# Low parts of the second feed-forward matrix: by an adding DMA in place of a subtraction on DVE

## The chip, the cores and the metric

The kernel runs on one core of one Trainium2 chip. The metric is the device time of one execution in microseconds (us). The core has a matrix engine (TensorE, PE, with its weight loads shown as PEld), a vector engine (VectorE, DVE), an activation engine (ScalarE, ACT), a general engine (GpSimd, POOL) and a synchronising engine (SyncE, SP) that issues most DMAs. Each engine works through its own list of instructions in order and waits for others by semaphores. Data lie in SBUF (128 partitions), matmul results in PSUM, weights in DRAM.

## The reference, cut to what matters

A trunk of two layers over 512 tokens with 1024 channels, all in float32. Each layer has four token mixers and then a feed-forward block, and the change is in the latter:

```
x = x + mixed @ w_out
h2 = rms_norm(x, norm_ff)
return x + jnp.square(jax.nn.relu(h2 @ w_ff1)) @ w_ff2      # w_ff1 [1024, 4096], w_ff2 [4096, 1024]
```

## The kernel before

**Three products for one.** PE multiplies in float32r, a shortened float32. To keep accuracy each operand is split in a high part (its float32r rounding) and a low part (what is left), and a product is the sum of high x high, low x high and high x low, added up in PSUM. So each block of weights is needed as `wh` (high) and `wl` (low).

**Weight chunks.** All weights are laid out in DRAM as one stream `w` of chunks [128, 1024] (512 KB), in the order of use. `chunk()` takes the next one. SP loads it into a raw buffer `wr` (three of them, `wr0` to `wr2`, in turn; seen as float32 they are called `wr0f`, as float32r `wr0r`). ACT copies it to `wh` (two buffers), which rounds it (line 275). DVE then writes raw - wh over the raw buffer (line 276): this is the low part.

**Use.** `mtile()` takes one chunk and makes 128 output channels for all 512 tokens: for k = 0 to 7 a matmul of `wh` with the high part of the activations, one of `wl` with the high part, and one of `wh` with the low part, 24 matmuls of 128x512. PE's order keeps these threes, so that the second matmul of a chunk is the first to need `wl`. In the trace both read as names of tiles: `ps<-yh,wh` or `ps<-yh,wr1r`.

**Feed-forward.** Four groups g in each layer. A group is 8 chunks of `w_ff1` (m = 0 to 7; relu and scale on DVE, line 475, square and high part on ACT, lines 476 and 478, low part on DVE, line 479) and then 8 chunks of `w_ff2`, whose results are added to x by DVE (line 485). That is 64 chunks of `w_ff2` in the program.

**What sets the order.** A scheduler writes each engine's list from the program's priorities and its own estimates of time; loads and splits of chunks have a raised priority. A load into a `wr` buffer waits until the chunk three before is done with on PE, a copy into a `wh` buffer until the one two before is. Beside the last group of `w_ff2` in layer 0 stand the first steps of layer 1's norm: ACT makes `hh` (line 370) and squares (line 338), POOL adds the squares (line 339). Beside that of layer 1 stand the squares of the last norm (line 388).

Of the kernel before, what the change touches and what calls it, by code (L numbers as in the profile page):

```python
# [32 lines left out]
# columns of the per-layer small pack  # L33
# [3 lines left out]
# columns of the constant pack  # L37
# [6 lines left out]
def fb(ap):  # L44
    return ap.bitcast(F32)


class Dual:
    """a buffer seen as float32 and as float32r"""
# [14 lines left out]
class Kern:  # L64
    def __init__(self, tc, A, out, depth, dbg=None):
        self.tc, self.nc, self.A, self.out, self.depth = tc, tc.nc, A, out, depth
        self.dbg = dbg or {}
        self.pools = []
        self.trace = None
        self.cidx = 0  # L70

# [110 lines left out]
    def setup_more(self):  # L182
# [24 lines left out]
        # second-pass key operands: rows 0-63 keys, then rows of -1 (64-95 or 96-127), zeros elsewhere  # L207
# [17 lines left out]
        # rope tables, rows as channels of two heads  # L225
# [29 lines left out]
    def order(self, a, b):  # L255
        """b after a on their engine"""
        self.tc.add_manual_dep(b.ins, a.ins.name,
                               mybir.DependencyInfo(mybir.DependencyClass.NoSync, mybir.DependencyReason.DATA),
                               reason="table order")
# [5 lines left out]
    def chunk(self, split=True):  # L265
        nc = self.nc
        i = self.cidx
        self.cidx += 1
        with self.tc.high_priority(4000 if i == 0 else 2000):
            raw = self.dual("wr")  # L270
            nc.sync.dma_start(raw.f[:], self.A["w"][i])
            if not split:
                return raw.f[:]
            wh = self.t("wh", 1024, F32R)
            nc.scalar.activation(wh[:], raw.f[:], AF.Copy)  # L275
            nc.vector.tensor_sub(raw[:], raw.f[:], fb(wh[:]))  # L276
        return wh, raw

    def mtile(self, xh, xl):
        """one tile of 128 output channels, transposed: [128 ch, 512 tok] in PSUM"""  # L280
        wh, wl = self.chunk()
        o = self.ps(self.dtag)
        n = len(xh)
        for k in range(n):
            s = slice(k * P, (k + 1) * P)
            self.mm(o[:], wh[:, s], xh[k][:], k == 0, False)
            self.mm(o[:], wl[:, s], xh[k][:], False, False)
            self.mm(o[:], wh[:, s], xl[k][:], False, k == n - 1)
        return o

    def mhalves(self, xh, xl):
        """mtile by halves of the tokens: (PSUM, tokens)"""
        wh, wl = self.chunk()
        for h in range(2):
            t = slice(h * 256, h * 256 + 256)
            o = self.ps(self.dtag, 256)
            for k in range(KT):
                s = slice(k * P, (k + 1) * P)
                self.mm(o[:], wh[:, s], xh[k][:, t], k == 0, False)
                self.mm(o[:], wl[:, s], xh[k][:, t], False, False)  # L300
                self.mm(o[:], wh[:, s], xl[k][:, t], False, k == KT - 1)
            yield o, t

    def vproducts(self, bank):
        """256 channels, token-major: two banks of two token tiles"""
        acc = [self.ps(bank) for _ in range(2)]
        for half in range(2):
            wh, wl = self.chunk()
            for k in range(4):
                for t in range(4):  # L310
                    o = acc[t // 2][:, (t % 2) * 256:(t % 2) * 256 + 256]
                    kk = half * 4 + k
                    s = slice(k * 256, (k + 1) * 256)
                    ts = slice(t * P, (t + 1) * P)
                    self.mm(o, self.hh[kk][:, ts], wh[:, s], kk == 0 and t % 2 == 0, False)
                    self.mm(o, self.hl[kk][:, ts], wh[:, s], False, False)
                    self.mm(o, self.hh[kk][:, ts], wl[:, s], False, kk == 7)
        return acc

    def vtiles(self, evac, acc=None):  # L320
        """evac(tok tile, psum [128 tok, 256 ch]) of the next 256 channels"""
        acc = acc or self.vproducts("d")
        with self.hi():
            for t in range(4):
                evac(t, acc[t // 2][:, (t % 2) * 256:(t % 2) * 256 + 256])

# [1 line left out]
    def rms(self, x, bank, early, in_psum=False):  # L328
        """x tiles -> 1/rms per token: [128, 512] (rows alike) and token-major [128, 4]"""
# [33 lines left out]
    def norm_split(self, x, gcol):  # L363
        """x * g as two parts; the tokens' 1/rms goes onto what is made of them"""
# [11 lines left out]
    def scaled(self, dst, o, scale=1.0):  # L376
        """dst = o * scale / rms"""
# [3 lines left out]
    def final(self, x):  # L381
        """the last norm; the last tile of channels comes in two halves of the tokens"""
# [36 lines left out]
    def layer(self, l, x):  # L419
# [5 lines left out]
        # the first products need no norm before they are written out  # L425
# [25 lines left out]
        # output projection  # L451
# [16 lines left out]
        for g in range(4):  # L468
            tags = rtags if g % 2 == 0 else rtags2
            RH, RL = [], []  # L470
            for m in range(8):
# [9 lines left out]
                RL.append(rl)  # L481
            for m in range(KT):
                last = l == self.depth - 1 and g == 3 and m == KT - 1
                for o, h in self.mhalves(RH, RL) if last else ((self.mtile(RH, RL), slice(0, S)),):
                    nc.vector.tensor_add(x[m][:, h], x[m][:, h], o[:])  # L485
        return x

    def ysplit(self, y):
        """y [128, 512] -> (high, low) tiles; the low part takes y's place"""
# [6 lines left out]
    def sigmoid(self, z):  # L496
        """in place, z at least -44"""
# [5 lines left out]
    def branch(self, n, qt):  # L503
        """mixed += sigmoid(gate_n + b) * (y_n @ W_branch_n), two tiles of channels"""
# [34 lines left out]
    def qk_pair(self, b_tiles=None):  # L539
        """project a pair of heads; per head (A, Q1, Q2) with  # L540
        head 0: A=[kh;kl], Q1=[qh;qh], Q2[0:64]=ql; head 1: A=[kl;kh], Q1=[qh;qh]; with b_tiles
        (rows 0-63 = kh) ql in Q2[0:64], else in the rows of kh"""
# [4 lines left out]
        out = []  # L547
# [11 lines left out]
    def kstack(self, k, A, B, b):  # L559
        """k on rows b*64..: its high part there in A, the low part in A's other half"""  # L560
# [7 lines left out]
    def regions(self, S3, win):  # L568
        """per key block: (psum AP, first query)"""
# [13 lines left out]
    def rowmax(self, S3, dst, win, negc=None):  # L583
        """column maxima of the masked scores; dst [32 rows, 512] gets diag(m)"""
# [35 lines left out]
    def probs(self, S3, win=False, bias=None, strict=False):  # L620
        """exp of the scores, masked; list of (AP, first query) per key block"""
# [19 lines left out]
    def pv(self, o, V, pr, start=True):  # L641
        """o [M, 512] += V_j^T P_j"""
# [3 lines left out]
    def recip(self, s, rows):  # L646
        """1/s for s [64 rows of PSUM], written at `rows`"""
# [7 lines left out]
    def v_plain(self, tag, c):  # L655
        """256 channels of values, token-major"""
# [6 lines left out]
    def sb_v(self, c, acc):  # L663
        """values of four heads, each as its high and low parts beside each other"""
# [17 lines left out]
    def sb_att(self, i):  # L682
        """scores with the queries on partitions, so that the sums over later keys are scans"""
# [3 lines left out]
        for b in range(2):  # L687
# [5 lines left out]
            # rows of 128 queries against all keys up to them: (bank, first column)  # L693
# [30 lines left out]
            # keys on partitions: (bank, first column) of a block of keys, queries from the same block on  # L724
# [27 lines left out]
    def vpair_evac(self, V, pair0):  # L752
        """token tile of 256 channels (4 heads) into [V0 | 1 | V1] groups of 192"""
# [15 lines left out]
    def small_proj(self):  # L769
        """nsa gates rows 0-23, gla decay rank rows 32-47, forget gate rows 64-71"""  # L770
# [16 lines left out]
        # gates of the three parts of the sparse attention, through DRAM to be read as rows alike  # L787
# [31 lines left out]
    def rope(self, o, scale, r=None):  # L819
        """rotated o * scale / rms, in r or in a tile of its own"""  # L820
# [11 lines left out]
    def compress_in(self, pecol):  # L832
        """two tiles [128 = (two positions, channel), 8 position pairs, 64 = (group, 31 blocks + pe)]"""
# [22 lines left out]
    def cmp_step(self, i, c):  # L856
        """a quarter of the first compression product"""
# [14 lines left out]
        if c == 3:  # L872
            # the position part
# [74 lines left out]
    def nsa(self, pi):  # L948
        """selected (here: all causal) and window attention of two heads"""
        nc = self.nc  # L950
        g, q, Ab, V = pi // 2, self.q, self.Ab, self.vnsa
        if True:
# [3 lines left out]
            for b in range(2):  # L956
# [7 lines left out]
                for br in range(2):  # L964
# [7 lines left out]
                    # [V|1] or [1|V] by the half the group's values sit in  # L972
# [17 lines left out]
    def nsa_cmp(self, g):  # L990
        """compressed attention of group g's four heads"""
# [40 lines left out]
    def gla_x(self, n, i):  # L1032
        """q (scaled) or k of two heads"""
# [7 lines left out]
    def gla_b(self, i):  # L1041
        """decays of two heads, summed within 64 tokens"""
# [25 lines left out]
    def gla(self, i):  # L1068
# [4 lines left out]
        if True:  # L1073
# [3 lines left out]
            # far pairs: products of decays from the middle of 512, 256 and 128 tokens  # L1077
# [47 lines left out]
            # pairs of one block of two tokens, the diagonal with them  # L1125
# [17 lines left out]
            # the other levels inside a block of 128 tokens; the two heads' queries beside each other,  # L1143
            # each with zeros at the other's channels
# [61 lines left out]
    def logsig(self, z, out):  # L1206
        """out = min(z, 0) - ln(1 + exp(-|z|))"""
# [10 lines left out]
def _kxm(w, c0):  # L1218
    """[K, 128 columns] -> [128, K/128 * 128]"""
# [11 lines left out]
# the token mixers' pieces in the order they are emitted: projections (with weights) and, in steps, attention  # L1231
# [142 lines left out]
```

## Time and profile before

| | |
|---|---|
| median of 3 runs | 2278.51 us (2278.09 to 2279.06) |
| profiled execution, span from first to last instruction | 2273.7 us |
| PE busy | 2230.2 us, 98% |
| DVE, ACT, POOL busy | 1488.2, 1035.6, 428.5 us |
| mean granted PE clock | 0.991 |
| DMA, mean | 90 GB/s |

The profile is one execution of the program. Its span leaves out what lies before the first and behind the last instruction, so it is 4.8 us below the median. Busy times of different engines overlap. A line of a group names the source line and engine, the tile written and the tiles read; behind "idle before" stands how long the engine stood still ahead of it, and which instruction ended that. Matmuls are pipelined, so that the time from one start to the next is shorter than the duration shown.

### The profile page before, as it was taken

The numbers are of one execution on the slowest core, as the hardware profiler recorded it, in microseconds if no ns is written. First come the engines' busy times: TensorE is split into PE (matmuls) and PEld (weight loads), VectorE is DVE, ScalarE is ACT, GpSimd is POOL, SyncE is SP. The second block draws the span as 40 slices with busy tenths as digits, with TensorE's granted clock in tenths as the row PEclk, the third lists the DMA queues.
The fourth block names the chain that finished last, engine by engine and source line by source line (L and its number), as shares of the span: only waits on it lengthen the run. The fifth ranks groups of instructions, "written<-read, shape, count | busy, mean of one in ns | idle before, by whom it ended". The sixth has DMA issues, their size and how long they took to land.

```text
span 2273.7 us, 28986 instructions
## 1 busy us (share of the span) xinstructions
PE 2230.2 (98%) x10740; PEld 1824.9 (80%) x10740; DVE 1488.2 (65%) x2434; ACT 1035.6 (46%) x1663; POOL 428.5 (19%) x759
## 2 busy tenths in 40 slices
PE   8999999999899999999999999999989999999998
PEld 7888878887788888888888888788868888888886
DVE  6889687888875444343458886978888654344344
ACT  5775544445544333232347654534454443232233
POOL 1223024434211200000112220234431112000000
PEclk9999999999999999999999999999999999999999
DMA  4222223322124332333432222233211243333332
GB/s 164 77 72 68 90 68 96 113 79 79 47 67 128 103 93 93 95 99 94 125 105 69 66 75 85 74 98 118 76 56 58 83 130 93 94 99 95 93 94 92
DMA packets 63108, 204.75 MB, mean 90 GB/s; under 512 B 7496, under 2 KB 10184, under 8 KB 62968
## 3 DMA queue, kind: packets, MB, share of 16 engines
q1 hardware_dynamic: 62968, 202.90, 29.1%
q8 instruction: 86, 1.41, 0.3%
q14 instruction: 54, 0.44, 0.1%
HBM read 198.57 MB, written 4.29 MB: 89 GB/s over the span
## 4 chain that ended last, share of the span: by engine, by line
PE 91%; DVE 5%; issue 1%; DMA 1%; ACT 1%; POOL 1%; POOLq 0%; DVEq 0%; SPq 0%; ACTq 0%
PE ps L121 48%; PE pd L121 42%; PE ps L730 1%; DMA wr1f<-in_w 0%; DMA wr0f<-in_w 0%; DVE sh L844 0%; POOL sm L613 0%; DVE wr1r L276 0%; DVE Q L616 0%; DVE m L1214 0%; DVE m L591 0%; DVE sx L609 0%; DVE m L605 0%; DVE Q L1109 0%; ACT wh L275 0%
## 5 line engine op out<-in xcount | busy, mean ns | idle before, releaser
L121 PE MATMUL pd<-hh,wh 128*128 128x512 f32 x1040 | 415.8, 400 | 0.2 <-ACT wh L275 0.2
L121 PE MATMUL pd<-hl,wh 128*128 128x512 f32 x1040 | 407.8, 392 | 0.0
L275 ACT ACTIVATE wh<-wr1f 128x1024 fp32r<-128x1024 f32 x112 | 118.7, 1060 | 274.7 <-PE ps L121 175.0
L275 ACT ACTIVATE wh<-wr0f 128x1024 fp32r<-128x1024 f32 x111 | 117.6, 1060 | 265.4 <-PE ps L121 176.3
L121 PEld LDWEIGHTS pd<-hh,wh 128*128 128x128 f32 x1040 | 195.6, 188 | 50.0 <-issue 4.0
L275 ACT ACTIVATE wh<-wr2f 128x1024 fp32r<-128x1024 f32 x111 | 117.6, 1060 | 256.9 <-PE ps L121 172.7
L121 PEld LDWEIGHTS pd<-hl,wh 128*128 128x128 f32 x1040 | 195.5, 188 | 42.2 <-issue 0.5
L121 PE MATMUL ps<-hh,wh 128*128 128x512 f32 x512 | 201.3, 394 | 0.0
L121 PE MATMUL ps<-hl,wh 128*128 128x512 f32 x512 | 199.3, 389 | 0.0
L276 DVE TENSOR_TENSOR wr0r<-wr0f,wh 128x1024 fp32r<-128x1024 f32 x111 | 143.4, 1292 | 43.0 <-ACT wh L275 42.5
L485 DVE TENSOR_TENSOR x<-x,ps 128x512 f32<-128x512 f32 (+1 forms) x65 | 44.2, 679 | 191.7 <-PE ps L121 191.7
L276 DVE TENSOR_TENSOR wr2r<-wr2f,wh 128x1024 fp32r<-128x1024 f32 x111 | 144.5, 1302 | 35.0 <-ACT wh L275 34.8
L121 PE MATMUL pd<-hh,wr2r 128*128 128x512 f32 x392 | 156.6, 400 | 0.0
L276 DVE TENSOR_TENSOR wr1r<-wr1f,wh 128x1024 fp32r<-128x1024 f32 x112 | 138.1, 1233 | 28.2 <-ACT wh L275 27.7
L475 DVE SCALAR_TENSOR_TENSOR p<-ps,rb 128x512 f32<-128x512 f32 x64 | 43.9, 691 | 157.3 <-PE ps L121 149.2
L121 PE MATMUL ps<-v,wh 128*128 128x512 f32 (+1 forms) x392 | 135.8, 389 | 0.0
L121 PE MATMUL pd<-hh,wr1r 128*128 128x512 f32 x336 | 134.4, 400 | 0.0
L121 PE MATMUL pd<-hh,wr0r 128*128 128x512 f32 x312 | 124.6, 399 | 0.0
L121 PE MATMUL ps<-p,v 128*128 128x384 f32 (+3 forms) x384 | 116.1, 426 | 2.2 <-POOL p L633 2.2
L121 PEld LDWEIGHTS ps<-hh,wh 128*128 128x128 f32 x512 | 96.1, 188 | 24.6 <-issue 0.5
L121 PE MATMUL pd<-yh,wh 128*128 128x512 f32 x256 | 105.0, 410 | 9.9 <-ACT yh L492 9.0
L121 PEld LDWEIGHTS ps<-hl,wh 128*128 128x128 f32 x512 | 96.2, 188 | 21.3
(638 smaller groups left out, 5326.8 us busy)
## 6 DMA issues: line engine op xcount, KB each, us to landing
wr0f<-in_w SPq DMA_DIRECT2D x117, 512.0 KB, 3.6
wr1f<-in_w SPq DMA_DIRECT2D x117, 512.0 KB, 3.6
wr2f<-in_w SPq DMA_DIRECT2D x116, 512.0 KB, 3.6
G<-gd SPq DMA_DIRECT2D x48, 128.0 KB, 3.1
x<-in_x SPq DMA_DIRECT2D x16, 256.0 KB, 3.5
xs<-x SPq DMA_DIRECT2D x8, 256.0 KB, 3.7
x<-xs SPq DMA_DIRECT2D x8, 256.0 KB, 3.3
out_y<-p SPq DMA_DIRECT2D x8, 256.0 KB, 2.4
```

Source lines behind the costliest of these rows:

```text
L121: i = self.nc.tensor.matmul(o, l, r, start=start, stop=stop, skip_group_check=True)
L275: nc.scalar.activation(wh[:], raw.f[:], AF.Copy)
L276: nc.vector.tensor_sub(raw[:], raw.f[:], fb(wh[:]))
L475: nc.vector.scalar_tensor_tensor(r[:], o[:], 0.0, self.rb[:], OP.max, OP.mult)
L485: nc.vector.tensor_add(x[m][:, h], x[m][:, h], o[:])
L730: nc.tensor.transpose(S3[n][:, c:c + P], at(F, q)[:, j * P:(j + 1) * P], self.ident)
```

## The change

The low part is wanted as raw - wh. For the chunks of `w_ff2` alone (the switch `dma_low`, set around the loop over them), ACT now writes -wh over the raw buffer, and POOL issues a DMA that reads the same chunk a second time from DRAM and adds it onto what the buffer holds. DVE's subtraction is gone for these 64 chunks; all others are made as before. The low part is finished when that DMA has landed. (The line numbers below line 70 move by one to eight; comments are dropped.)

```diff
@@ class Kern, __init__
+        self.dma_low = False
@@ weights
-    def chunk(self, split=True):
+    def chunk(self, split=True, dma_low=False):
...
             wh = self.t("wh", 1024, F32R)
             nc.scalar.activation(wh[:], raw.f[:], AF.Copy)
-            nc.vector.tensor_sub(raw[:], raw.f[:], fb(wh[:]))
+            if dma_low:
+                nc.scalar.activation(raw[:], fb(wh[:]), AF.Copy, scale=-1.0)
+                nc.gpsimd.dma_start(raw[:], self.A["w"][i].bitcast(F32R), accum_op=OP.add)
+            else:
+                nc.vector.tensor_sub(raw[:], raw.f[:], fb(wh[:]))
         return wh, raw
@@ mtile and mhalves
-        wh, wl = self.chunk()
+        wh, wl = self.chunk(dma_low=self.dma_low)
@@ layer, the loop over the chunks of w_ff2
+            self.dma_low = True
             for m in range(KT):
...
+            self.dma_low = False
```

On ACT, at the start of the `w_ff2` chunks of layer 0's first group, the rows of before are these (`wh_961` and so on are high parts, `p_957` the activations of the last `w_ff1` chunks but one, the rows from L478 their high parts):

```order
L275 ACTIVATE wh_961_7196<-wr2f_59 128x1024
L476 ACTIVATE p_957_7156<-p_957_7156 128x512
L478 ACTIVATE e1r_76<-p_957_7156 128x512
L275 ACTIVATE wh_963_7226<-wr0f_55 128x1024
L476 ACTIVATE p_960_7190<-p_960_7190 128x512
L478 ACTIVATE e3r_80<-p_960_7190 128x512
L275 ACTIVATE wh_965_7256<-wr1f_57 128x1024
L275 ACTIVATE wh_967_7286<-wr2f_59 128x1024
```

Of after, at the same place on ACT (L276 is the copy now, L279 the negation, L482 the square, L484 the high part):

```order
L276 ACTIVATE wh_961_7196<-wr2f_59 128x1024
L482 ACTIVATE p_957_7156<-p_957_7156 128x512
L279 ACTIVATE wr2r_60<-wh_961_7196 128x1024
L484 ACTIVATE e1r_76<-p_957_7156 128x512
L276 ACTIVATE wh_963_7227<-wr0f_55 128x1024
L482 ACTIVATE p_960_7190<-p_960_7190 128x512
L279 ACTIVATE wr0r_56<-wh_963_7227 128x1024
L484 ACTIVATE e3r_80<-p_960_7190 128x512
L276 ACTIVATE wh_965_7258<-wr1f_57 128x1024
L279 ACTIVATE wr1r_58<-wh_965_7258 128x1024
L276 ACTIVATE wh_967_7289<-wr2f_59 128x1024
L279 ACTIVATE wr2r_60<-wh_967_7289 128x1024
```

One negation follows each copy; for a group's first two chunks a square stands between the two.

On POOL, in layer 0's last group, the additions of the next norm's squares (`m`, `p`) stood behind each other in the program of before:

```order
L345 TENSOR_TENSOR rt_928_6909<-rt_928_6909,mhalf_120 128x4
L339 TENSOR_TENSOR m_1142_9254<-m_1142_9254,p_1143_9256 128x512
L339 TENSOR_TENSOR m_1142_9254<-m_1142_9254,p_1144_9259 128x512
L339 TENSOR_TENSOR m_1142_9254<-m_1142_9254,p_1145_9262 128x512
L339 TENSOR_TENSOR m_1142_9254<-m_1142_9254,p_1146_9265 128x512
L339 TENSOR_TENSOR m_1142_9254<-m_1142_9254,p_1147_9268 128x512
```

In the program of after POOL has the DMAs, here the last seven of layer 0's 32, and between them the same additions (L345 now):

```order
L280 DMA wr0r_56<-in_w 128x1024
L280 DMA wr1r_58<-in_w 128x1024
L345 TENSOR_TENSOR m_1142_9286<-m_1142_9286,p_1143_9288 128x512
L280 DMA wr2r_60<-in_w 128x1024
L345 TENSOR_TENSOR m_1142_9286<-m_1142_9286,p_1144_9291 128x512
L280 DMA wr0r_56<-in_w 128x1024
L345 TENSOR_TENSOR m_1142_9286<-m_1142_9286,p_1145_9294 128x512
L280 DMA wr1r_58<-in_w 128x1024
L345 TENSOR_TENSOR m_1142_9286<-m_1142_9286,p_1146_9297 128x512
L280 DMA wr2r_60<-in_w 128x1024
L345 TENSOR_TENSOR m_1142_9286<-m_1142_9286,p_1147_9300 128x512
L280 DMA wr0r_56<-in_w 128x1024
```

Each of these five additions now stands ahead of a DMA. On PE the order inside a chunk of `w_ff2` is the same in both programs, and so is SP's order of loads.

## Rows read from the trace of the kernel before

**Rows 1.** The page's first part: busy us, share of the span, instructions.

```profile
span 2273.7 us, 28986 instructions
PE 2230.2 (98%) x10740; PEld 1824.9 (80%) x10740; DVE 1488.2 (65%) x2434; ACT 1035.6 (46%) x1663; POOL 428.5 (19%) x759
```

**Rows 2.** Chain that ended last, 780 to 1140 us: start, us, what.

```profile
by line: PE ps L121 99.6%; PE pd L121 0.5%
...
798.22 341.86 PE ps L121 x1495
```

**Rows 3.** Waits of PE, whole run: us in total, times, longest us.

```profile
PE pd L121 <- DVE wr2r L276: 0.4, 1, 0.4
...
PE ps L121 <- DVE wr1r L276: 0.3, 1, 0.3
```

**Rows 4.** Timeline of SP, second product, layer 0: start, us, engine, instruction.

```profile
1014.74 0.33 SPq L271 DMA_DIRECT2D wr2f<-in_w  x1
1020.25 0.33 SPq L271 DMA_DIRECT2D wr0f<-in_w  x1
```

**Rows 5.** Timeline of ACT, same group; in brackets idle time before and its end.

```profile
998.38 1.06 ACT L275 ACTIVATE wh<-wr1f 128x1024 fp32r<-128x1024 f32 x1 [3.30 <-PE ps L121]
999.34 0.61 ACT L476 ACTIVATE p<-p 128x512 f32<-128x512 f32 x1
999.99 0.63 ACT L478 ACTIVATE e0r<-p 128x512 fp32r<-128x512 f32 x1
...
1014.97 1.06 ACT L275 ACTIVATE wh<-wr1f 128x1024 fp32r<-128x1024 f32 x1 [1.91 <-PE ps L121]
```

**Rows 6.** Timeline of DVE, the same chunk.

```profile
1016.06 1.23 DVE L276 TENSOR_TENSOR wr1r<-wr1f,wh 128x1024 fp32r<-128x1024 f32 x1 [0.41 <-ACT wh L275]
```

**Rows 7.** Timeline of PE: a group's first chunk, then the chunk of rows 6.

```profile
1003.96 0.39 PE L121 MATMUL ps<-yh,wr1r 128*128 128x512 f32 x1
...
1020.29 0.40 PE L121 MATMUL ps<-yh,wh 128*128 128x512 f32 x1
1020.52 0.39 PE L121 MATMUL ps<-yh,wr1r 128*128 128x512 f32 x1
```

**Rows 8.** Lines 276 and 275, whole run: ns min/median/max of one.

```profile
L276 DVE TENSOR_TENSOR wr1r<-wr1f,wh x112: 1195/1224/2318, 17.8 to 2250.0; 128x1024 fp32r<-128x1024 f32 x112
...
L275 ACT ACTIVATE wh<-wr1f x112: 1042/1060/1087, 15.2 to 2248.9; 128x1024 fp32r<-128x1024 f32 x112
```

**Rows 9.** Busy us (PE, PEld, DVE, ACT, POOL), PE clock, DMA share, GB/s.

```profile
1000.00:1100.00 100.00, 100.00 (x435) 81.46 (x434) 39.78 (x45) 29.04 (x36) 0.00 (x0) 1.00 0.31 97
```

**Rows 10.** Timelines of ACT and POOL, layer 0's last group.

```profile
1104.49 0.71 ACT L370 ACTIVATE hh<-x,small 128x512 fp32r<-128x512 f32 x1
1105.10 0.61 ACT L338 ACTIVATE p<-x 128x512 f32<-128x512 f32 x1
...
1105.85 1.80 POOL L339 TENSOR_TENSOR m<-m,p 128x512 f32<-128x512 f32 x1 [313.91 <-issue]
```

**Rows 11.** DMA issues: count, KB each, median us from issue to landing.

```profile
wr1f<-in_w SPq DMA_DIRECT2D x117, 512.0 KB, 3.6
...
x<-in_x SPq DMA_DIRECT2D x16, 256.0 KB, 3.5
...
out_y<-p SPq DMA_DIRECT2D x8, 256.0 KB, 2.4
```

**Rows 12.** Timeline of PE, layer 0's mixers.

```profile
561.94 0.50 PE L121 MATMUL pd<-yh,wh 128*128 128x512 f32 x1 [1.62 <-ACT yh L492]
...
563.57 0.85 PE L121 MATMUL ps<-Q,B 128*128 128x384 f32 x4 [0.89 <-DVE Q L616]
```

**Rows 13.** Busy us, PE clock (third from the end), DMA, behind rows 12.

```profile
564.00:565.00 1.00, 0.88 (x6) 0.64 (x5) 1.00 (x4) 0.95 (x3) 0.39 (x1) 0.94 1.00 403
565.00:566.00 1.00, 1.00 (x4) 0.81 (x3) 1.00 (x8) 0.88 (x3) 1.00 (x3) 0.50 0.41 129
...
568.00:569.00 1.00, 1.00 (x5) 0.73 (x4) 1.00 (x6) 0.97 (x2) 0.00 (x0) 0.85 0.00 0
```

More of the change, by code (lines that the diff above doesn't have):

```diff
@@ L291, in mhalves @@
     def mhalves(self, xh, xl):
-        wh, wl = self.chunk()
+        wh, wl = self.chunk(dma_low=self.dma_low)
         for h in range(2):
```

## The prediction, made before the changed kernel had run

> **What bounds the kernel now.** I read the page's first part first: TensorE (PE) is busy for 2230.2 of 2273.7 us and no other engine passes 65% [rows 1]. Then the chain that ended last, for the feed-forward part of layer 0: in 780 to 1140 us it is PE from end to end, with one unbroken piece of 341.86 us [rows 2]. So in the stages that the change touches there is only one way to save time, fewer PE microseconds, and the change takes none away. What can happen is that PE starts to wait. The next view is therefore the list of what PE waited for: the low parts made by VectorE (DVE) stand there with 0.3 to 0.4 us for each of their three buffers in the whole run [rows 3]. A faster or idler DVE has about 1 us to give.
>
> Next, the rhythm. The loads of one weight chunk in the second feed-forward product are issued at 1014.74 and 1020.25 [rows 4]: one chunk (24 matmuls) is 5.51 us. A load into a buffer is issued when the chunk three before it is done, so these are also the times at which chunks end.
>
> Last, the preparation of one chunk, the one that PE begins at 1020.29. There are two `wh` buffers, so its high part can only be copied when the chunk two before it is done: that chunk ends at 1014.74, ACT's copy begins at 1014.97 and takes 1.06 [rows 5]. DVE's subtraction follows at 1016.06 and takes 1.23 [rows 6], so the low part is there at 1017.29. PE's first matmul of the chunk (high part) starts at 1020.29, its second, the first that reads the low part, at 1020.52 [rows 7]. Slack today: 1020.52 - 1017.29 = 3.2 us.
>
> **Removed and added, on the engines.** DVE loses 64 subtractions (2 layers x 4 groups x 8 chunks) of 1.22 us median [rows 8], 78 us of work. PE does not wait for it there, so this is worth 0. If it were the cover of anything, it would be of the 1 us in [rows 3]. ACT gains 64 activations of the same 128x1024 form as its copy, 1.06 us each [rows 8], 68 us; it idles some 70 of 100 us in this stage [rows 9], so its load costs nothing by itself. What counts is that the new steps stand in a row behind the copy.
>
> **The new chain.** Copy 1014.97 to 1016.03. One ACT instruction after another that reads its result starts 0.04 later (0.61 us Square ends 999.95, next starts 999.99) [rows 5], so the negation is 1016.07 to 1017.13, no later than DVE's result today. Then POOL is told: a POOL instruction that waited for ACT began 0.14 after ACT's end (1105.71 to 1105.85) [rows 10], so the DMA is issued at 1017.27. PE wants the low part at 1020.52. The DMA therefore has **3.25 us** from issue to landing before PE stands still. Call its time T; a chunk waits T - 3.25.
>
> For the first chunk of a group, ACT's order in the changed program puts a Square (0.61) between copy and negation. From [rows 5]: copy 998.38, Square to 999.95, negation to 1001.05, issue 1001.19; its second matmul starts at 1003.96 [rows 7]. That leaves 2.77, so it waits T - 2.75.
>
> How many chunks pay? A chunk that waits delays its successor, and with it gives the successor the same time for its own DMA: the successor's `wh` was free 5.5 us after the first one's, and it now starts that much later plus the wait. So waits come at every second chunk: four in a group of eight, one of T - 2.75 and three of T - 3.25. PE's order inside a chunk (high, low, high, repeated) is unchanged in mid-group, so nothing fills the gap beyond the one first matmul that I have counted.
>
> **T, bounded.** No DMA issued by POOL, and none that adds, is in this trace. The nearest row is the plain load of the same 512 KB: 3.6 us to landing [rows 11]. Adding must read the destination too. The engines move 97 GB/s at a busy share of 0.31 [rows 9], so 313 GB/s when busy, and 512 KB take 1.7 us of the 3.6. One more stream of bytes: 5.3. POOL's own issue I price like SP's, 0.33 [rows 4]: **T = 5.7** is what I take. The lower end for an add is the plain load, 3.6. The upper end is two plain loads behind each other, 7.2, with the longest POOL instruction of the neighbourhood, 1.80 [rows 10], ahead of them: 9.0. A collision with the raw load of a later chunk, which is in flight for 3.6 us out of each 5.5, lies within that.
>
> A page speaks against this sum. The Trainium skill, DMA: Bandwidth & Descriptors, section "Anatomy of one DMA — SWDGE (gpsimd) path", fits a POOL-issued DMA as 2.0 us plus bytes over 436 GB/s. By that page 512 KB would be an estimated 3.2 us, less than this trace's 3.6 for a load from SP, and the loss would all but vanish. The fit is for copies; Collectives: The Full Stack, section "The bandwidth ceiling", says that an add needs two source reads on one ring and halves the rate. No run here yet shows either, and the sum goes by the rows.
>
> **The sum.** At T = 5.7 a group waits 2.95 + 3 x 2.45 = 10.3 us; 8 groups, 82 us.
>
> Two groups pay more. In layer 0's last group ACT has the next norm's two activations before the negation (0.71 and 0.61, hence 1.25 later), and POOL an addition of 1.80 ahead of the DMA, which begins 0.14 after ACT's and so holds the DMA another 0.84 [rows 10]: 1.25 + 2.1 + 2.1 over its three later waits, 5.4 us. In layer 1's last group one Square (0.61) stands there: 3 x 0.65 = 2.0. Together 7.4 us.
>
> **The clock.** PE's granted clock falls after idle time. In layer 0 at 560 to 564 us PE idled 1.62 and 0.89 us between short bursts [rows 12], and then ran at 0.50 (1.2 instead of 2.4 GHz): the clocks of 564 to 569 lack 0.06 + 3 x 0.50 + 0.15 = 1.7 us of full speed [rows 13]. A wait of 2.45 us in one piece is as much idle time. I take it that two waits of three bring a fall, 1.1 us each: 32 x 1.1 = 35 us. Bounds: 0 (none falls) and 54 (all do).
>
> Layer 1's mixers are also emitted in a slightly other order in places, since the scheduler that writes the order counts with other times; I put 0 +- 4 us on that.
>
> Sum: 82 + 7 + 35 = 124 us on a span of 2273.7. The three runs have a median of 2278.5, so 4.8 us lie outside that span and stay. Forecast **2403 us**.
>
> **The rivals.**
> - *The add is priced like a load* (T 2.9 to 4.4). At 3.6: 8 x (0.85 + 3 x 0.35) = 15, plus 7, no fall of the clock: 2301. At 4.4 with half of the falls: 41 + 7 + 16, 2343. For it: the load's 3.6 is the only row. Against it: the second stream. The page's fit would be T = 3.2 and, by this mechanism, 8 x 0.45 = 4 us and some 7 in the two late groups: 2289. Chance with all of this case: 0.16.
> - *The adding DMA is much slower* (T over 7.5): 140 + 7 + 48 = 195 at 7.5, 2474; at 9.0, 188 + 7 + 54, 2528. For it: nothing in the trace shows how long POOL takes to issue a DMA, or at what rate one adds. Chance 0.17.
> - *Not slower.* The low part lands before PE asks: decided at T = 2.7, the point from which all waits together stay under 0.2% (4.6 us). The nearest row is the store of 256 KB, 2.4 [rows 11]; then only layer 0's last group waits, some 3 us, 2281. Against it: loads of half the size already take 3.5. Chance 0.05, of which 0.02 for a gain: DVE's freed time could speed the layer's transitions.
> - *The change does not do what it says*: the built program has the 64 DMAs on POOL and 64 fewer subtractions on DVE, so I give this nothing.
>
> **Chances and range.** Forecast case (T 4.4 to 7.5, 2343 to 2474): 0.62. The time given is its middle. For 8 in 10 I leave out the lower half of the first rival and what lies above T = 9: 2320 to 2530. A measurement here tells some 0.2% from nothing. Slower by more: 0.95; within: 0.03; faster: 0.02.
>
> **What will show it.** (1) PE's list of waits has the low part's DMA, `wr` from `in_w`, some 32 times, near 2.5 us each, at every second chunk; the chain that ended last in the feed-forward stages passes through that DMA, POOL and ACT in place of PE alone. (2) The DMA issues list a POOL group of 64 with 512 KB; its landing time is T, and decides by how much I am off: each 1 us of T is 32 us. (3) The loads are 5.5 and some 8 to 9.5 us apart in turn. (4) The granted clock in 780 to 1140, now 1.00, falls to about 0.9. (5) DVE's 39.8 us in 100 of that stage [rows 9] go below 30, with no gain. Wrong would be: no PE waits there (T under 3.25), or waits at each chunk and not at every second, which would double the sum.

## The result and the profile after

The changed kernel takes **2406.42 us** (median of 3 runs, 2398.66 to 2409.55) against 2278.51: a ratio of 1.056 (95% interval 1.053 to 1.058). The forecast was 2403, in a range of 2320 to 2530. The profiled execution is the one of 2409.55, with a span of 2407.9 us, 134.2 more than before's.

The page's first part, to be read beside [rows 1]: DVE's 64 subtractions are gone as planned, ACT and POOL have 64 instructions more each, and PE's share falls from 98 to 95%.

```profile
span 2407.9 us, 29291 instructions
PE 2276.8 (95%) x10740; PEld 1849.7 (77%) x10740; DVE 1412.2 (59%) x2370; ACT 1099.8 (46%) x1727; POOL 484.1 (20%) x823
```

The waits of PE (us in total, times, longest), all lines in which it stands ahead of a matmul that reads a low part of `w_ff2`, but for one wait of 0.3 us. In [rows 3] the waits for low parts in the whole run were 0.3 to 0.4 for a buffer.

```profile
PE ps L122 <- ACT wr1r L279: 23.5, 9, 2.9
PE ps L122 <- ACT wr0r L279: 22.8, 9, 2.8
PE ps L122 <- ACT wr2r L279: 17.6, 7, 2.8
...
PE ps L122 <- ACT x L397: 6.4, 2, 3.5
...
PE ps L122 <- ACT sh L484: 2.9, 1, 2.9
PE ps L122 <- ACT e2r L484: 2.9, 1, 2.9
PE ps L122 <- DMA wr0r<-in_w: 2.5, 1, 2.5
PE ps L122 <- DMA wr2r<-in_w: 2.3, 1, 2.3
PE ps L122 <- DMA wr1r<-in_w: 2.1, 1, 2.1
```

That is 83.0 us in 32 waits. Most lines name ACT, but ACT had been done long before, as one pair of chunks shows. Its rows, from the timelines of ACT, POOL, PE and SP (start, us, engine, instruction, idle before and its end), answer [rows 4 to 7]:

```profile
1050.17 1.06 ACT L276 ACTIVATE wh<-wr0f 128x1024 fp32r<-128x1024 f32 x1 [7.42 <-PE ps L122]
1051.27 1.07 ACT L279 ACTIVATE wr0r<-wh 128x1024 fp32r<-128x1024 f32 x1
```

```profile
1052.63 0.86 POOL L280 DMA_DIRECT2D wr0r<-in_w  x1 [9.24 <-ACT wr0r L279]
```

```profile
1058.28 0.47 PE L122 MATMUL ps<-yh,wr0r 128*128 128x512 f32 x1 [2.57 <-ACT wr1r L279]
1072.18 0.48 PE L122 MATMUL ps<-yh,wr2r 128*128 128x512 f32 x1 [2.63 <-ACT wr0r L279]
```

```profile
1063.65 0.33 SPq L272 DMA_DIRECT2D wr0f<-in_w  x1
1069.16 0.33 SPq L272 DMA_DIRECT2D wr1f<-in_w  x1
1077.55 0.33 SPq L272 DMA_DIRECT2D wr2f<-in_w  x1
```

Copy, negation, DMA: ACT ends at 1052.34, POOL issues the DMA at 1052.63, and PE goes on at 1058.28, 5.65 later. The list names the last event on a semaphore, and for the wait at 1058.28 that is ACT's negation of another buffer. That the DMA ends the waits can be read from its landings: by the trace it landed at 1058.19 here, and each of the 32 waits ends 0.04 to 0.09 us after the landing of the DMA that made its low part. The loads, which follow the ends of chunks, are 5.5 and 8.4 us apart in turn: every second chunk waits. The DMA issues (count, KB, median us to landing) tell how long the new step takes:

```profile
wr0f<-in_w SPq DMA_DIRECT2D x117, 512.0 KB, 3.6
...
wr0r<-in_w POOLq DMA_DIRECT2D x22, 512.0 KB, 5.7
wr2r<-in_w POOLq DMA_DIRECT2D x21, 512.0 KB, 5.6
wr1r<-in_w POOLq DMA_DIRECT2D x21, 512.0 KB, 5.6
```

The chain that ended last, 1050 to 1070 us, was PE alone in [rows 2]; now it leaves PE for the copy and the negation. It follows the same last event as the list of waits, the negation of the next chunk, so that the DMA, which really ended the wait, shows only as 0.61 of "issue":

```profile
1055.51 1.06 ACT wh L276
...
1056.60 1.06 ACT wr1r L279
1057.66 0.61 issue
1058.28 11.05 PE ps L122 x47
```

Busy us of PE, PEld, DVE, ACT and POOL, granted clock, DMA share and GB/s: the first row answers [rows 9], the next ones [rows 13] at one wait of layer 0.

```profile
1000.00:1100.00 100.00, 89.43 (x378) 71.60 (x377) 26.17 (x32) 34.25 (x40) 6.92 (x8) 0.98 0.53 126
```

```profile
844.00:845.00 1.00, 0.00 (x0) 0.00 (x0) 0.17 (x1) 0.97 (x2) 0.00 (x0) 1.00 1.07 213
845.00:846.00 1.00, 0.00 (x0) 0.00 (x0) 0.00 (x0) 0.63 (x1) 0.07 (x1) 0.91 0.95 295
846.00:847.00 1.00, 0.88 (x2) 0.81 (x3) 0.00 (x0) 0.00 (x0) 0.79 (x1) 0.50 0.73 295
847.00:848.00 1.00, 1.00 (x4) 0.71 (x4) 0.00 (x0) 0.00 (x0) 0.00 (x0) 0.50 0.89 78
848.00:849.00 1.00, 1.00 (x4) 0.81 (x3) 0.00 (x0) 0.00 (x0) 0.00 (x0) 0.50 0.89 131
849.00:850.00 1.00, 1.00 (x6) 0.77 (x5) 0.00 (x0) 0.00 (x0) 0.00 (x0) 0.88 0.85 168
```

From the end of this wait on (PE starts again at 846.12) the granted clock is 0.50 (1.2 in place of 2.4 GHz) for some 3.4 us: the rows lack 0.09 + 3 x 0.50 + 0.12 = 1.71 us of full speed. Not every wait does this: behind the waits of 1058 and 1072 the clock stays.

**Where the 134.2 us are.** I measure a feed-forward stage from its first relu row on DVE to the start of its last addition to x. Layer 0, before and after:

```profile
798.89:1136.80 337.91, 337.91 (x1467) 274.93 (x1466) 143.36 (x163) 109.20 (x139) 11.35 (x9) 1.00 0.33 101
```

```profile
800.14:1203.92 403.78, 360.26 (x1467) 285.71 (x1466) 105.15 (x131) 140.74 (x171) 36.26 (x41) 0.95 0.53 126
```

That is +65.9 us; layer 1 goes from 338.01 to 401.31, +63.3. The mixers of layer 0 give +1.25, those of layer 1 +3.7. Within the two stages, 129.2 us:

- Low-part waits: 83.0 listed, and 0.17 more at each, since the matmul ahead of a wait is 0.40 long in a slot of 0.23 and so covers the gap's beginning: 88.44.
- In layer 0's last group PE stands three times for a copy as well (0.91 each, and the 0.17): 3.24.
- Clock: over windows of 1 us the stages lack 0 us of full speed before and 37.5 after, 22 steps of 1.7.

Together 129.2. Some 2.1 us of the clock's loss lie inside the waits and are counted in both, so the sum closes to about 2 us.

### The profile page after: what moved, and what is told of

Read it like the earlier page. It is cut to its first block, busy times and chain, and to the rows that moved or that the text cites. A ratio compares the mean times of both kernels' runs of the same rounds, so it can differ in the third digit from the quotient of the medians.

```text
span 2407.9 us, 29291 instructions
## 1 busy us (share of the span) xinstructions
PE 2276.8 (95%) x10740; PEld 1849.7 (77%) x10740; DVE 1412.2 (59%) x2370; ACT 1099.8 (46%) x1727; POOL 484.1 (20%) x823
## 4 chain that ended last, share of the span: by engine, by line
PE 87%; DVE 5%; ACT 4%; DMA 2%; issue 2%; POOL 1%; SPq 0%; POOLq 0%; DVEq 0%; ACTq 0%
PE ps L122 46%; PE pd L122 40%; ACT wh L276 2%; PE ps L738 1%; ACT wr1r L279 0%; DMA wr0f<-in_w 0%; ACT wr0r L279 0%; DMA wr1f<-in_w 0%; ACT wr2r L279 0%; DVE wr1r L282 0%; DMA wr0r<-in_w 0%; DMA wr1r<-in_w 0%; DMA wr2r<-in_w 0%; POOL sm L621 0%; DMA x<-in_x 0%
## 5 line engine op out<-in xcount | busy, mean ns | idle before, releaser
L276 ACT ACTIVATE wh<-wr1f 128x1024 fp32r<-128x1024 f32 x112 | 118.8, 1060 | 295.2 <-PE ps L122 194.0
L276 ACT ACTIVATE wh<-wr0f 128x1024 fp32r<-128x1024 f32 x111 | 117.7, 1061 | 296.9 <-PE ps L122 201.3
L276 ACT ACTIVATE wh<-wr2f 128x1024 fp32r<-128x1024 f32 x111 | 117.7, 1060 | 275.0 <-PE ps L122 193.4
L122 PE MATMUL ps<-v,wh 128*128 128x512 f32 (+1 forms) x392 | 146.6, 418 | 2.7 <-ACT wh L276 2.7
L282 DVE TENSOR_TENSOR wr0r<-wr0f,wh 128x1024 fp32r<-128x1024 f32 x89 | 116.8, 1312 | 33.9 <-ACT wh L276 33.5
L282 DVE TENSOR_TENSOR wr2r<-wr2f,wh 128x1024 fp32r<-128x1024 f32 x90 | 119.5, 1328 | 26.5 <-ACT wh L276 26.2
L282 DVE TENSOR_TENSOR wr1r<-wr1f,wh 128x1024 fp32r<-128x1024 f32 x91 | 112.4, 1236 | 18.8 <-ACT wh L276 18.4
L544 POOL TENSOR_TENSOR mixed<-mixed,gt 128x512 f32<-128x512 f32 x48 | 67.9, 1418 | 247.2 <-DVE gt L542 246.0
L641 POOL TENSOR_SCALAR_AFFINE_SELECT p<-p 128x128 f32<-128x128 f32 x192 | 82.2, 448 | 161.1 <-ACT p L640 159.5
```

The lines of the kernel that those rows point to most:

```text
L122: i = self.nc.tensor.matmul(o, l, r, start=start, stop=stop, skip_group_check=True)
L544: nc.gpsimd.tensor_add(self.mixed[m][:], self.mixed[m][:], g)
L641: nc.gpsimd.affine_select(d[:, 0:P], d[:, 0:P], [[1, P]], OP.is_gt if strict else OP.is_ge, 0.0, base=0, channel_multiplier=-1)
```

## Experiments

Each time is the median of 3 to 13 executions, and each ratio is to executions of the kernel before that were taken beside them. Stage lengths (layer 0 + layer 1) are taken as above; T is the median time of the POOL-issued DMA from issue to landing.

| kernel | time, us | ratio to before (95%) | feed-forward stages, us | T, us |
|---|---|---|---|---|
| before | 2275 to 2279 | | 337.9 + 338.0 | |
| changed | 2406.42 | 1.0556 (1.0530 to 1.0582) | 403.8 + 401.3 | 5.6 |
| aside | 2281.14 | 1.0024 (1.0015 to 1.0034) | 339.4 + 339.6 | 5.6 to 5.8 (two of 256 KB) |
| plain | 2316.34 | 1.0173 (1.0157 to 1.0189) | 359.4 + 356.5 | 3.9 |
| half | 2322.73 | 1.0204 (1.0187 to 1.0221) | 361.0 + 361.7 | 4.0 |
| lowlast | 2305.65 | 1.0130 (1.0106 to 1.0155) | 357.9 + 357.6 | 6.7 |
| wh3 | 2344.11 | 1.0294 (1.0277 to 1.0312) | 378.0 + 369.9 | 6.9 |
| raw6 | 2408.15 | 1.0572 (1.0553 to 1.0591) | 405.2 + 401.7 | 5.6 |
| raw6_lowlast | 2288.61 | 1.0051 (1.0036 to 1.0066) | 342.1 + 342.6 | 7.4 |
| raw6_wh3 | 2304.01 | 1.0128 (1.0111 to 1.0146) | 350.8 + 350.0 | 5.8 |
| mix100 | 2298.62 | 1.0097 (1.0082 to 1.0113) | 337.9 + 338.0 | 6.3 |

**The work, or the chain?** My theory: the negation and the DMA cost nothing as work; what costs is that they stand in the chain behind the two `wh` buffers. The rival is that they disturb (ACT's load, DMA traffic). *aside* does the added work beside the path and lets DVE make the low part:

```diff
-                nc.scalar.activation(raw[:], fb(wh[:]), AF.Copy, scale=-1.0)
-                nc.gpsimd.dma_start(raw[:], self.A["w"][i].bitcast(F32R), accum_op=OP.add)
+                nc.vector.tensor_sub(raw[:], raw.f[:], fb(wh[:]))
+                for j in range(2):
+                    sc = self.t(("G", "gt", "Q2")[i % 3])
+                    cs = slice(j * 512, j * 512 + 512)
+                    nc.scalar.activation(sc[:], fb(wh[:, cs]), AF.Copy, scale=-1.0)
+                    nc.gpsimd.dma_start(sc[:], self.A["w"][i][:, cs], accum_op=OP.add)
```

> All that the change adds is done for the 64 chunks of w_ff2, but beside the path: DVE subtracts as before, while ACT writes -wh into scratch tiles and POOL issues DMAs that add the same 512 KB (in two halves of 256 KB) onto these; nobody reads the scratch. Theory (PE waits for a chain of copy, negation, POOL and DMA that is longer than a chunk): 2279 to 2290 us, no waits of PE in the feed-forward stages, clock 1.00 there. Rival (the added work costs by itself: 33.5 MB more traffic delays the loads, ACT or POOL is overloaded): 2320 to 2410, with raw loads landing clearly later than 3.6 us.

Measured: 2281.14, with the stages 3.0 us longer in all, no wait of PE listed in them, a clock of 1.00 there and loads still at 3.6 in the median. The same traffic and the same ACT work cost 3 of the 129 us.

**How much of T is the adding?** *plain* has the same chain with a DMA that writes, and *half* adds half of the columns:

```diff
 plain
-                nc.gpsimd.dma_start(raw[:], self.A["w"][i].bitcast(F32R), accum_op=OP.add)
+                nc.gpsimd.dma_start(raw[:], self.A["w"][i].bitcast(F32R))
 half
+                nc.gpsimd.dma_start(raw[:, 0:512], self.A["w"][i][:, 0:512].bitcast(F32R), accum_op=OP.add)
```

> As the changed kernel, but POOL's DMA writes the weights over the buffer instead of adding them (so the low part holds the weights themselves; the sum of products is another one). It tells what adding costs within T. If the second stream of bytes is the cost, T falls from 5.6 to about 4.1 (the load's 3.6 and some 0.5 for POOL's issue), the waits from 2.8 to 1.3 us, fewer falls of the clock: 2320 to 2345 us. Rival (POOL's issue and the fixed part make T): T stays above 5.2, 2385 to 2406. Rival (as a page has it for copies): T 3.2, waits below 0.5 us, 2285 to 2300.

> As the changed kernel, but POOL's DMA adds only the first 512 of 1024 columns (the low parts of the other half are left at -wh, so the sum of products is another one). T against size, and the waits against T. If T is a fixed part and two streams of bytes: 5.65 - 1.7 = 3.9 to 4.0, waits some 1.1 us, hardly a fall of the clock: 2310 to 2325 us, as for the plain write of 512 KB, which had T 3.9. Rival (adding costs per transfer, not per byte): T above 5, 2385 or more.

The DMA issues of *plain*, then of *half*:

```profile
wr0r<-in_w POOLq DMA_DIRECT2D x22, 512.0 KB, 3.9
```

```profile
wr0r<-in_w POOLq DMA_DIRECT2D x22, 256.0 KB, 4.0
```

A write of 512 KB takes 3.9, an add of 512 KB 5.6, an add of 256 KB 4.0. So 256 KB of adding are 1.6 us, and a fixed part of some 2.4 is left. If a write has the same fixed part, which no run tested, it has 1.5 for 512 KB, and adding moves the bytes at an estimated half of its rate. That is the second stream of the prediction (1.7). The Trainium skill, Collectives: The Full Stack, "The bandwidth ceiling", states for the add of a collective that its two source reads on one ring halve the rate, and the runs here agree. By the fit of the Trainium skill, DMA: Bandwidth & Descriptors, "Anatomy of one DMA — SWDGE (gpsimd) path", a copy of 512 KB would take an estimated 3.2 us, where *plain* shows 3.9.

*plain* came out below its expected time and *half* at the upper end; neither has a fall of the clock in the stages. *plain*'s stages are 40.0 us longer, 1.25 on average over 32 waits. Against it the changed kernel has 1.7 us more T and 91.7 - 40.0 = 51.7 us more waits, 1.6 for each: a microsecond of T costs some 30 us, as forecast (32).

**Can the chain be covered?** Two kernels were to give the DMA more time. In *lowlast* PE does a chunk's 16 high-part matmuls first and the 8 low ones last; *wh3* has three `wh` buffers (as halves of 512 columns):

```diff
 lowlast, in mtile
+        if self.dma_low:
+            for k in range(n):
+                s = slice(k * P, (k + 1) * P)
+                self.mm(o[:], wh[:, s], xh[k][:], k == 0, False)
+                self.mm(o[:], wh[:, s], xl[k][:], False, False)
+            for k in range(n):
+                s = slice(k * P, (k + 1) * P)
+                self.mm(o[:], wl[:, s], xh[k][:], False, k == n - 1)
+            return o
 wh3, in chunk
+                ha, hb = self.t("Q1", 512, F32R), self.t("qk", 512, F32R)
+                nc.scalar.activation(ha[:], raw.f[:, 0:512], AF.Copy)
+                nc.scalar.activation(hb[:], raw.f[:, 512:1024], AF.Copy)
+                nc.scalar.activation(raw[:, 0:512], fb(ha[:]), AF.Copy, scale=-1.0)
+                nc.scalar.activation(raw[:, 512:1024], fb(hb[:]), AF.Copy, scale=-1.0)
```

> As the changed kernel, but for w_ff2 the 16 matmuls of a chunk that read the high part come first, the 8 that read the low part last. The low part is wanted 15 matmuls x 0.23 = 3.5 us later, and the high buffer is free up to 8 matmuls = 1.8 us sooner. Theory: the measured wait of 2.8 us is covered by either, so no waits: 2279 to 2290 us. Rival (traffic, ACT or POOL are the cost, wherever the low part is read): stays near 2400. Rival (the adding DMA itself slows PE): near 2400 too, with slower matmuls.

> As the changed kernel, but the high parts of w_ff2 go into three buffers (each in two halves of 512 columns, copied and negated by two ACT instructions each) instead of two. Theory (the two wh buffers start the chain too late): the chain has 5.5 us more; then the third raw buffer is the next limit: its load is issued at the end of the chunk three before, lands 3.7 later, then copy 1.2, negation 1.2, POOL 0.3, DMA 5.7: 12.1, against 11.5 from there to the matmul that needs it; some 0.6 us at every third chunk, 13 us, with hardly a fall of the clock: 2285 to 2310 us. Rival (the rate of POOL or of the DMA limits, not the buffer): 2380 to 2410.

Both missed. Of 129 us of loss they give back 90 and 57, then something else waits. In *lowlast* the copy, which had always waited for PE, waits for the raw load at 39 of the 64 chunks, and in *wh3* PE waits for the DMA 34 times, by 1.3 us on average. Rows of *lowlast* (timeline of ACT), then of *wh3* (waits of PE):

```profile
1026.79 1.06 ACT L276 ACTIVATE wh<-wr1f 128x1024 fp32r<-128x1024 f32 x1 [4.47 <-DMA wr1f<-in_w]
```

```profile
PE ps L133 <- DMA wr2r<-in_w: 18.9, 13, 2.4
PE ps L133 <- DMA wr0r<-in_w: 16.6, 13, 2.5
```

And T rose to 6.7 and 6.9. The new theory: the ring of three raw buffers is the next limit. A raw buffer is taken from the issue of its load to the chunk's end; 3.6 for the load, 2.5 for copy, negation and issue, 6.9 for the DMA and 5.5 for the chunk are 18.5 us, and three buffers at one chunk each 5.5 us allow 16.5. This sum is *wh3*'s, whose loads into one buffer lie 17.8 to 20.9 us apart in the first three groups of layer 0. In *lowlast* the low part is read only in the last 8 matmuls, some 2 us in place of the 5.5, and the sum comes to no more than 15; it is the trace that shows the limit there, with loads that take up to 7.5 us and lie 15.6 to 21.1 us apart for one buffer in the same groups. *raw6* gives `w_ff2` six raw buffers of its own, alone and with the order of *lowlast* (some activations move to other tiles, to make room):

```diff
+        for i in range(6):
+            f = nc.alloc_sbuf_tensor_at(f"wx{i}f", [P, 1024], F32, offset=base)
+            r = nc.alloc_sbuf_tensor_at(f"wx{i}r", [P, 1024], F32R, offset=base)
+            bufs.append([f, r, None])
...
-            raw = self.dual("wr")
+            raw = self.dual("wx" if dma_low else "wr")
```

> As the changed kernel, but the raw chunks of w_ff2 go into six buffers of their own (memory that is free in this stage) instead of three; two wh buffers and PE's order as in the changed kernel. It parts the two rings. Theory (the wh ring starts the chain and alone sets the waits here): 2385 to 2410 us, 32 waits near 2.8 us, T 5.6. Rival (the raw ring sets them, as it did where wh was relieved): 2280 to 2310.

> Six raw buffers and, in w_ff2, the matmuls that read the low part last. Theory (after the wh ring, the raw ring of three was the next limit: load 3.6, copy, negation and POOL 2.5, adding DMA 5.6 to 6.9, use 5.5 or more, together above 3 x 5.5 = 16.5): with six there is no wait left, 2276 to 2290 us, the feed-forward stages 338 to 342 us each. Rival (loads and adding DMAs slow each other, whatever the buffers): 2295 to 2310, T near 6.8 and PE's waits for low parts still there.

Both as the ring theory has it. *raw6* alone changes nothing (2408.15): in the changed kernel the two `wh` buffers set the waits. With both, the stages are 342.1 and 342.6 us, 4.2 and 4.6 above before's, although T is 7.4 in the median: the chain is long, but PE hardly waits for it (five waits are left, 0.8 us at most). What 100 us of the stage look like then, beside 89.43 of PE and a clock of 0.98 above:

```profile
1000.00:1100.00 100.00, 99.24 (x428) 79.99 (x427) 28.04 (x35) 39.25 (x47) 7.79 (x9) 1.00 0.57 137
```

Open after that: do more buffers do it, or was the order of the matmuls needed, since loads and adding DMAs in flight together stretch each other? *raw6_wh3* has six raw buffers and three of high parts (the two edits above, with other tiles for the halves and the activations), with PE's order as in the changed kernel.

> The changed kernel with six raw buffers for the second feed-forward matrix and with three buffers of high parts (as halves of 512 columns), TensorE's order of matmuls left as it is in the changed kernel. Theory, two rings: the ring of high parts sets the waits of the changed kernel (six raw buffers alone left it at 2408.15 us), and with three buffers the ring of raw chunks took over (2344.11 us with three); relieved of both, a chunk's low parts may land 5.5 us later than now, which covers an adding DMA of up to 7.5 us beside loads: hardly a wait for low parts, each feed-forward stage 338 to 346 us, 2280 to 2300 us in all. Rival, the DMA's rate: an adding DMA and a load in flight together slow each other until TensorE waits whatever the buffers, and only the reordered matmuls hid that in the run with low parts last (2288.61): waits of about 2 us at every second chunk stay, feed-forward stages of 360 us or more, 2320 to 2345 us.

Measured 2304.01, 4 above the theory's range and 16 below the rival's. PE's low-part waits in layer 0's stage, all of them:

```profile
PE ps L141 <- DMA wx3r<-in_w: 3.5, 2, 2.0
PE ps L141 <- DMA wx1r<-in_w: 2.2, 1, 2.2
PE ps L141 <- DMA wx5r<-in_w: 1.5, 1, 1.5
```

Four of them in layer 0 and four in layer 1, one in each group in place of four: from the fifth chunk of a group on the buffers cover the chain, as the theory says. The wait that is left stands at each group's fourth chunk. For the third group, from the timelines of SP, POOL and PE:

```profile
1018.29 0.33 SPq L291 DMA_DIRECT2D wx4f<-in_w  x1
1020.12 0.33 SPq L291 DMA_DIRECT2D wx5f<-in_w  x1
```

```profile
1020.86 0.86 POOL L300 DMA_DIRECT2D wx1r<-in_w  x1 [53.00 <-ACT wx1r L299]
1022.57 0.86 POOL L300 DMA_DIRECT2D wx2r<-in_w  x1 [0.85 <-ACT wx2r L299]
```

```profile
1028.82 0.50 PE L141 MATMUL ps<-yh,wx1r 128*128 128x512 f32 x1 [2.23 <-DMA wx1r<-in_w]
```

The two loads tell that the group's first two chunks end 1.8 us apart and not 5.5, so less time is left up to the fourth. Its DMA took 7.9 us, beside these loads and the next adding DMA; with 5.6 it would have landed at 1026.5, just before PE stood at 1026.59. So the rival's point is right here: the slower DMA makes this wait. At all eight waits that DMA took 7.1 to 8.0.

**Is DVE's freed time worth something elsewhere?** DVE is busier in the mixers (76% of the time before) than in the feed-forward stages (42%). *mix100* makes low parts by DMA for the later GLA projections and gates and branch gates of the mixers (low matmuls last, as above), and those of `w_ff2` by DVE. By the trace that is 23 chunks in a layer, not the 14 of the expectation:

```diff
-        for it in MIXERS:
+        for im, it in enumerate(MIXERS):
             f = getattr(self, it[0])
+            self.dma_low = im in MIXLOW and it[0] in ("gla_gate", "gla_x", "branch")
```

> The other place for the same means: w_ff2 as in the kernel before (DVE subtracts), and the adding DMA for the chunks of the GLA gates and projections and of the branch gates that come after position 100 of the mixers, 14 in a layer, with the low parts read last. There DVE is busy all the time and PE waits for what it makes. Theory (DVE's 1.2 us per chunk is on the path there): PE waits less, 2250 to 2275 us. Rival (the longer way of a low part makes new waits there): 2280 to 2320.

Measured 2298.62: the feed-forward stages are back at before's length, and the mixers are 17.6 and 10.1 us longer: PE stands still 10.2 and 7.9 us more in them, and their clock lacks 6.8 and 1.7 us more. Which of the moved steps makes PE wait was not taken apart. For this choice of chunks DVE's time bought nothing; another choice was not tried. None of these kernels is faster than the one before.

## Why the prediction was right, point by point

**The place and the pattern** held: 32 waits, four in a group, at every second chunk, with ACT in the chain; that DMA and POOL would show there did not hold, for the reason given with its rows. *aside* and *raw6_lowlast* show that the chain's place costs, and not its work. DVE's relief (39.78 to 26.17 us in 100) brought no gain, as stated.

**T** was taken as 5.7 (its terms, 3.6, 1.7 and 0.33, add up to 5.63) and is 5.6, and its part for adding (1.7) is what *plain* leaves out. For the fixed part the sum had the right size by luck: it put POOL's issue at 0.33 on a load's 3.6, and *plain*'s 3.9 agrees; the POOL instruction itself is 0.86 long. The rival "priced like a load" falls with that: it is true of *plain*, whose DMA does not add.

**Time before PE stands**: 3.25 was a little too long. POOL's start behind ACT is 0.29 (1052.34 to 1052.63), where 0.14 had been read from [rows 10], and PE goes on 0.04 to 0.09 after the landing. Outside the two last groups the 26 waits sum to 71.1 us, with the hidden 0.17; the forecast for them was 8 x 2.95 + 18 x 2.45 = 67.7.

**The two late groups** were over-sized in layer 0: three waits of 10.7 in all, those for copies included, 12.75 forecast. POOL's addition took 1.29 and not the 1.80 of [rows 10], so it held the DMA some 0.15 in place of 0.84. The cause can be read: before, that addition ran beside a DVE instruction that reads two tiles of SBUF, and after, beside 0.1 us of it. The DVE row of before, then POOL and DVE after:

```profile
1105.76 0.75 DVE L371 SCALAR_TENSOR_TENSOR hl<-x,small,hh 128x512 fp32r<-128x512 f32 x1
```

```profile
1168.82 1.29 POOL L345 TENSOR_TENSOR m<-m,p 128x512 f32<-128x512 f32 x1 [8.82 <-ACT p L344]
```

```profile
1168.17 0.75 DVE L377 SCALAR_TENSOR_TENSOR hl<-x,small,hh 128x512 fp32r<-128x512 f32 x1 [1.02 <-ACT hh L376]
```

The Trainium skill, SBUF — State Buffer, "Who interferes with whom", states that such a DVE instruction contends with a POOL instruction that reads SBUF; the two durations agree. No experiment was made for it, but the same additions in the other runs bear it out: with 0.64 us beside such an instruction they take 1.79, with 0.37 (one in *plain*) 1.53, with 0 to 0.12 between 1.26 and 1.30. In these the DVE instruction had started first. Where POOL had (*lowlast*, at 1157.86 and 1160.00), it took 1.30 and 1.39 although DVE ran beside it for longer, and the DVE instruction that came second took 1.54 in place of 1.22, and 1.77 in place of 0.75. Layer 1's late group was forecast at 9.35 for three waits and had 9.9. The errors offset, which is luck: 91.7 us of waits in all, 89 forecast.

**The clock**: 35 forecast, 37.5 measured. Its working was coarser than that looks. "Two of three waits, 1.1 on average" came out as 22 steps of 1.7 at 32 waits; which waits bring a fall was not forecast, and waits of like length (2.44 at 846, 2.57 at 1058) differ in it. That the total came so near is in part luck: in *half* waits of up to 2.1 us and in *wh3*'s layer 1 waits of up to 2.5 brought no fall, while in *lowlast* one of 1.9 did.

**The mixers** gave +1.25 and +3.7, where 0 +- 4 had been put on layer 1's; their clock lacks 3.4 us more in layer 1. The points named as signs hold, except the list and the chain, as said, and that the clock over 780 to 1140 is 0.96 and not some 0.9: 35 us spread over two stages of 400 are 0.045, which the forecast's own sum could have told.

## What to carry to other kernels

An instruction taken from an engine that nobody waits for is worth nothing, and what takes its place is to be priced by where it stands: put the new steps in a row behind the buffer that starts them, up to the first reader, and compare with the time of one round of each ring of buffers. If the row is too long, one more buffer moves the wait to the next ring; count all rings (here `wh` and raw) and the place of the first reader before building.

## What the runs showed of the hardware

- An adding DMA issued by POOL, DRAM onto SBUF: 5.6 us for 512 KB and 4.0 for 256 KB, against 3.9 for a write of 512 KB.
- Loads and adding DMAs in flight together take longer. In *raw6_lowlast* the loads of `w_ff2` in layer 0 had medians of 4.3 to 8.1 us by buffer in place of 3.6, and T rose to 7.4; in *aside* two adding DMAs of 256 KB behind each other took 5.6 to 5.8 each in the median, where one alone (*half*) takes 4.0. Whether by a shared rate or by an order in the queues was not settled.
- A fall of PE's clock cost 1.7 us or twice that, each time: 22 such steps in 19 falls at the changed kernel's 32 waits of 2.1 to 3.5 us, none in the stages of *plain*, whose waits are 1.3 us at most. The length of a wait alone did not decide it.
- A POOL addition of two SBUF tiles of 128x512 took 1.26 to 1.30 us, and 1.79 when it started behind a DVE instruction with two SBUF inputs that ran on beside it for 0.64 us.
